# Scratch places by the plan's clock, new booked durations, and five weight halves with three raw blocks, in a hybrid decoder step

## The chip, the cores and the metric

The kernel runs on 1 core of one Trainium2 chip. The metric is device microseconds of one execution; lower is better. The engines are TensorE (PE in the profile, with its weight loads as PEld), VectorE (DVE), ScalarE (ACT), GpSimd (POOL), and SyncE (SP), which issues the DMA transfers here.

## The reference

One layer of a decoder, in float32, over 304 columns: 16 meta tokens, a prompt of 256 tokens, and 8 sequences of 4 new tokens each. Cut to what is computed:

```python
def decoder_layer(x, ...):
    xn = rms_norm(x, norm_mix)
    z = xn @ w_in                                  # 2048 -> 3360 RWKV columns + 4096 retention columns
    z_a, z_b = z[..., :RWKV_COLS], z[..., RWKV_COLS:]
    z_prev = concat([shift0, z_a[:, :-1]])
    o_a, S_a = rwkv7_mixer(z_a, z_prev, ...)       # 16 heads of 64, a state of 64x64 per head
    o_b, S_b = retention_mixer(z_b, ...)           # 4 heads of 256, a state of 256x256 per head
    h = x + concat([o_a, o_b]) @ w_out             # 2048 -> 2048
    hn = rms_norm(h, norm_ffn)
    return h + (silu(hn @ w_gate) * (hn @ w_up)) @ w_down    # 2048 -> 5632 -> 2048
```

A final norm follows. Returned are the outputs without the meta tokens, the last projected row, and both kinds of state, for the prompt and for each of the 8 sequences. The RWKV recurrence is solved in chunks of up to 64 tokens, the retention in chunks of 128, so both turn into many small matmuls between the large projections.

## The kernel before

**Projections.** Activations lie transposed, 128 channels on the partitions and up to 304 tokens along the row. Each projection is a list of output tiles of 128 columns, in the order that `sequence` (line 101) and `ORDER` give: the loras, then eight pairs of RWKV heads and four retention heads mixed, their gates, the output projection in two halves, then gate, up and down of the FFN. A tile sums over up to 16 steps of 128 rows. Every step is three matmuls in the rounded float32 format: high weight half by high activation half, high by low, low by high. They accumulate in one of two PSUM banks named `acc`; all other small matmuls write one of six banks named `mm`.

**Weights.** All weights are one array, `big`, packed in the order of use in raw blocks of 128 x 1024. `load` issues one block (512 KB) into a ring of `WR` buffers named `wr`; in `start` the first four blocks are issued as eight half blocks between the pieces of the input. `cast` rounds 512 columns on ACT to a tile `wh`, and `rest` lets DVE subtract that from the raw values to give `wl`; each of these has `WS` buffers. One half of 512 columns serves four steps, twelve matmuls. `main` (line 609 on) writes the steps of all projections in order; at each half it calls `load` until `WR` blocks from the present position are asked for, and `cast` until `WS - 1` halves from there are asked for:

```python
while self.loaded < min(total, at + WR * WCOLS):
    self.load()
while self.halved < min(total, at + (1 if starting else WS - 1) * 512):
    self.cast()
```

The subtracts are written at the middle of a half (`o == 256`), or at the next half's start if that half needs them.

**The planner.** The work between projections is written as generators (`mixed`, `pair`, `inverse`, `units`, `sample`, `pair_out`, `ret`, ...) that yield where they would wait. The program is written twice. The first pass is a draft: `Plan.book` gives every instruction a duration, follows values through tiles, and keeps a clock per engine; `Plan.pick` lets a generator take its next step once the clock of TensorE has passed the time when its last step was done. The choices are logged and replayed in the second pass, which writes the real program. So the booked durations set the order in which each engine's instructions stand, and each engine runs its list in order. `put` and `flush` issue output stores some 20 us of the plan's clock after they are asked for. The draft knows of the rings `wr`, `wh`, `wl`, `acc` and `mm` (`follows`), but gives each scratch tile words of its own.

**Scratch.** In the second pass all scratch tiles are pieces of two large tiles, the arenas, one of float32 and one of the rounded type (`arena_dt.float` and `arena_dt.float32r` in the profile). `Room` decides which words each tile gets. It notes for every tile the count of booked instructions when it was made and when it was last used; `pack` sorts the tiles by a key and gives each the lowest place that no tile with an overlapping life (longer by `slack` instructions) holds; `place` tries five keys, keeps the smallest room, and goes from a slack of 40 down to 0 until the room fits. Together the two rooms may hold 33,000 words per partition (`ROOM`), 4,200 of them of the rounded type. Where two tiles follow each other on the same words, the new owner's first instruction waits until the old owner's last reader is done. That holds for loads too, and SyncE issues its DMAs in order.

Every operation is recorded through one helper, so all rows of the profile name line 300; the tiles tell them apart.

Of the kernel before, what the change touches and what calls it, by code (L numbers as in the profile page):

```python
# [41 lines left out]
LATE = 20000  # L42
WARM = 10
BRIDGE = 4
WR = 4
WCOLS = 1024
WS = 4
PAIRS = 2
PMAX = 3
AHEAD = 2  # L50
# [25 lines left out]
KEYS = ((0, META, SEQ, 0), (P, P, NP - P, SEQ), (LASTK, 2 * P, T - 2 * P, SEQ + NP - P))  # L76
RMW = SEQ + NP - P + T - 2 * P
ROOM = 33000


def zcols():
# [223 lines left out]
class Plan:  # L305
# [5 lines left out]
    def __init__(self, nc, rooms, draft, log, keep):  # L311
        self.keep = keep
        self.rooms, self.draft, self.log, self.count = rooms, draft, log, 0
        self.clock = dict(PE=0.0, DVE=0.0, ACT=0.0, POOL=0.0, SP=0.0)
        self.end = self.dma = 0.0
        self.uses, self.outside = {}, ()
# [29 lines left out]
    def book(self, eng, what, a, k):  # L346
        self.count += 1
        if not self.draft:
            return
        aps = [x for x in (*a, *k.values()) if hasattr(x, "shape")]  # L350
        for x in aps:
            for room in self.rooms.values():
                room.use(x, self.count)
        out, ins = aps[0], aps[1:]

        at = 0.0
        boxes = [(x.name, self.box(x), x is out) for x in aps if x.name not in self.outside]
        meet = lambda a, b: a[0] < b[1] and b[0] < a[1] and a[2] < b[3] and b[2] < a[3]
        for name, box, writes in boxes:
            for other, done, by, written in self.uses.get(name, ()):  # L360
                if (written or writes) and done + 100 > at and not (by == eng == "PE") and meet(box, other):
                    at = max(at, done + (30 if by == eng else 100 if eng == "PE" else 60))
        n = math.prod(out.shape[1:])
        if eng == "PE":
            done = self.array(what, *a[:3], at) + 170
        elif eng == "SP":
            self.clock[eng] = at = max(self.clock[eng] + 400, at)
            self.dma = max(self.dma, at + 1400) + 4 * out.shape[0] * n / 320
            done = self.dma + 600
        else:  # L370
            part = out.shape[0] < P
            if eng == "DVE":
                big = max(math.prod(x.shape[1:]) for x in aps)
                dur, tail = {"stream_shuffle": (148, 90), "transpose": (95 + 1.02 * n, 80), "tensor_reduce": (40 + 1.8 * big, 85),
                             "tensor_tensor_scan": (65 + 2.1 * n, 85)}.get(what, (62 + 1.05 * n, 83))
            elif eng == "ACT":
                dur, tail = 108 + 0.83 * n, 94
            else:
                dur, tail = (60 + 0.85 * n, 60) if what == "memset" else (260 + 2.4 * n, 60)
            if part and eng != "POOL":  # L380
                dur += 110
# [72 lines left out]
class Room:  # L454

    def __init__(self):
        self.spans, self.index, self.places, self.size, self.taken = [], {}, None, 0, 0

    def note(self, ap, size, count):
        self.index[ap.name] = len(self.spans)
        self.spans.append([size, count, count])

    def use(self, x, count):
        i = self.index.get(getattr(x, "name", None))
        if i is not None:
            self.spans[i][2] = count

    def place(self, limit):  # L470


        for slack in (40, 20, 10, 5, 0):
            best = None
            for key in (lambda n, a, b: (-n, a), lambda n, a, b: (-n * (b - a), a), lambda n, a, b: (a - b, -n),
                        lambda n, a, b: (a, -n), lambda n, a, b: (-n // 256, a - b)):
                size, places = self.pack(key, slack)
                if best is None or size < best[0]:
                    best = size, places
            if best[0] <= limit:  # L480
                break
        self.size, self.places = best
        assert self.size <= limit, self.size

    def pack(self, key, slack):
        done, places = [], [0] * len(self.spans)
        for i in sorted(range(len(self.spans)), key=lambda i: key(*self.spans[i])):
            size, a, b = self.spans[i]
            size = -(-size // 8) * 8
            b += slack  # L490
            at = 0
            for o, n, c, d in sorted(x for x in done if x[2] <= b and a <= x[3]):
                if o - at >= size:
                    break
                at = max(at, o + n)
            places[i] = at
            done.append((at, size, a, b))
        return max(o + n for o, n, _, _ in done), places

    def take(self, size):  # L500

# [14 lines left out]
class Step:  # L516
# [33 lines left out]
    def t(self, shape, tag, dt=F32, bufs=None, pool=None):  # L550
        self.n += 1
        if pool is not None:
            name = f"{tag}_{self.n}"
            old = self.tags.setdefault(tag, [])
            old.append(name)
            n = {"mm": 8 - ACC, "acc": ACC}.get(tag, bufs)
            if n and len(old) > n:
                self.plan.follows(name, old[-1 - n])
            return pool.tile(shape, dt, tag=tag, name=name, **({} if bufs is None else {"bufs": bufs}))
        size = math.prod(shape[1:])  # L560
        if self.draft:
            ap = self.mp.tile(shape, dt, tag=f"t{self.n}", name=f"{tag}_{self.n}")
            self.rooms[dt].note(ap, size, self.plan.count)
            return ap
        o = self.rooms[dt].take(size)
        flat = self.arena[dt][:shape[0], o:o + size]
# [1145 lines left out]
def body(tc, I, O):  # L1712
# [32 lines left out]
```

## Time and profile before

| what | value |
|---|---|
| median of the runs | 1593.91 us (1592.52 to 1594.58, 3 runs) |
| the profiled execution's own time | 1595.29 us |
| its span, first to last instruction | 1593.5 us |
| mean granted clock of TensorE | 0.996 |
| busy: PE, DVE, ACT, POOL | 1547.0, 1101.9, 822.2, 166.5 us |
| moved by DMA | 252.49 MB, 158 GB/s on average |

Times in the profile are microseconds from the first instruction unless marked ns. A row of a group gives engine, operation, tiles written and read, shape and count, then busy time, mean ns of one, and the idle time of the engine just before them with what ended it. A row of waits reads: who waited, for whom, us in total, times, the longest. A row by stretches gives busy us and instruction counts of each engine, the granted clock, the busy share of the DMA engines and GB/s. Matmuls are pipelined, so the drawn length of one is longer than its distance to the next.

### The profile page before, as it was taken

The numbers are of one execution on the slowest core, as the hardware profiler recorded it, in microseconds if no ns is written. First come the engines' busy times: TensorE is split into PE (matmuls) and PEld (weight loads), VectorE is DVE, ScalarE is ACT, GpSimd is POOL, SyncE is SP. The second block draws the span as 40 slices with busy tenths as digits, with TensorE's granted clock in tenths as the row PEclk, the third lists the DMA queues.
The fourth block names the chain that finished last, engine by engine and source line by source line (L and its number), as shares of the span: only waits on it lengthen the run. The fifth ranks groups of instructions, "written<-read, shape, count | busy, mean of one in ns | idle before, by whom it ended". The sixth has DMA issues, their size and how long they took to land.

```text
span 1593.5 us, 30795 instructions
## 1 busy us (share of the span) xinstructions
PE 1547.0 (97%) x11388; PEld 1506.5 (95%) x11388; DVE 1101.9 (69%) x2590; ACT 822.2 (52%) x1795; POOL 166.5 (10%) x567
## 2 busy tenths in 40 slices
PE   9999999999999999999999999999999999999997
PEld 8888999898888899999999999999999999999997
DVE  7888888897879867777565656565655656565657
ACT  6657676747656564455444444444444444444445
POOL 0343414323041300000000000000000000000000
PEclk9999999999999999999999999999999999999998
DMA  7443343334543448655555555555555555555553
GB/s 263 144 123 112 114 126 113 101 113 133 157 156 117 143 149 278 231 163 157 169 164 165 168 170 159 169 166 168 166 166 172 160 165 167 172 162 170 162 168 116
DMA packets 76998, 252.49 MB, mean 158 GB/s; under 512 B 9392, under 2 KB 14640, under 8 KB 76848
## 3 DMA queue, kind: packets, MB, share of 16 engines
q1 hardware_dynamic: 76848, 250.52, 50.8%
q8 instruction: 90, 1.47, 0.4%
q14 instruction: 60, 0.49, 0.1%
HBM read 236.21 MB, written 14.28 MB: 157 GB/s over the span
## 4 chain that ended last, share of the span: by engine, by line
PE 71%; DVE 6%; DMA 2%; ACT 1%; issue 1%; POOL 1%; DVEq 0%; POOLq 0%; ACTq 0%; SPq 0%
PE acc L300 66%; PE mm L300 5%; DVE arena_dt.float L300 5%; DVE wl L300 1%; ACT arena_dt.float L300 1%; DMA arena_dt.float<-s0r 1%; POOL arena_dt.float L300 1%; DMA arena_dt.float<-lora 1%; DVE arena_dt.float32r L300 0%; ACT wh L300 0%; DVE xl L300 0%; ACT arena_dt.float32r L300 0%; DVEq L1741 0%; POOL shout L300 0%; POOLq L300 0%
## 5 line engine op out<-in xcount | busy, mean ns | idle before, releaser
L300 PE MATMUL acc<-xh,wh 128*128 128x288 f32 (+2 forms) x2592 | 791.7, 305 | 0.6 <-ACT wh L300 0.6
L300 PE MATMUL acc<-xh,wl 128*128 128x288 f32 (+2 forms) x2592 | 772.8, 298 | 13.3 <-DVE wl L300 13.2
L300 PE MATMUL acc<-xl,wh 128*128 128x288 f32 (+2 forms) x2592 | 766.8, 296 | 0.0
L300 ACT CAST wh<-wr 128x512 fp32r<-128x512 f32 x826 | 500.9, 617 | 363.8 <-PE acc L300 327.7
L300 DVE TENSOR_TENSOR wl<-wr,wh 128x512 fp32r<-128x512 f32 x826 | 562.8, 689 | 127.8 <-ACT wh L300 124.8
L300 PEld LDWEIGHTS acc<-xh,wl 128*128 128x128 f32 x2592 | 486.1, 188 | 19.7 <-DVE wl L300 18.9
L300 PEld LDWEIGHTS acc<-xh,wh 128*128 128x128 f32 x2592 | 487.8, 188 | 5.9 <-issue 1.3
L300 PEld LDWEIGHTS acc<-xl,wh 128*128 128x128 f32 x2592 | 486.9, 188 | 3.7 <-issue 0.5
L300 PE MATMUL acc<-arena_dt.float32r,wh 128*128 128x288 f32 x1408 | 280.0, 294 | 0.4 <-ACT arena_dt.float32r L300 0.3
L300 PEld LDWEIGHTS acc<-arena_dt.float32r,wh 128*128 128x128 f32 x1408 | 226.3, 188 | 0.9 <-ACT arena_dt.float32r L300 0.6
L300 PE MATMUL acc<-arena_dt.float32r,wl 128*128 128x288 f32 x704 | 208.0, 295 | 0.0
L300 DVE TENSOR_TENSOR arena_dt.float<-acc,arena_dt.float 128x288 f32<-128x288 f32 (+4 forms) x181 | 72.8, 420 | 167.1 <-PE acc L300 166.2
L300 PE MATMUL mm<-arena_dt.float 128*128 128x128 f32 (+6 forms) x1072 | 172.0, 311 | 15.4 <-ACT arena_dt.float L300 5.9
L300 PEld LDWEIGHTS mm<-arena_dt.float 128*128 128x128 f32 (+1 forms) x1072 | 138.1, 181 | 32.7 <-ACT arena_dt.float L300 8.5
L300 DVE TENSOR_TENSOR arena_dt.float<-arena_dt.float 128x288 f32<-128x288 f32 (+10 forms) x483 | 158.5, 355 | 10.8 <-ACT arena_dt.float L300 4.3
L300 DVE TENSOR_TENSOR arena_dt.float<-arena_dt.float,acc 128x288 f32<-128x288 f32 x208 | 94.4, 454 | 100.4 <-PE acc L300 99.9
L300 ACT ACTIVATE arena_dt.float<-arena_dt.float 128x288 f32<-128x288 f32 (+6 forms) x200 | 85.2, 433 | 122.7 <-DVE arena_dt.float L300 115.5
L300 ACT COPY arena_dt.float<-mm 64x64 f32<-64x64 f32 (+11 forms) x330 | 91.7, 286 | 80.6 <-PE mm L300 74.9
L300 PEld LDWEIGHTS acc<-arena_dt.float32r,wl 128*128 128x128 f32 x704 | 132.4, 188 | 0.0
L300 ACT CAST arena_dt.float32r<-arena_dt.float 128x288 fp32r<-128x288 f32 (+4 forms) x73 | 30.4, 423 | 124.2 <-DVE arena_dt.float L300 92.6
L300 POOL TENSOR_TENSOR arena_dt.float<-arena_dt.float 128x75 f32<-128x75 f32 (+14 forms) x240 | 86.9, 362 | 73.1 <-DVE arena_dt.float L300 50.1
L300 POOL MEMSET arena_dt.float<- 128x64 f32 (+8 forms) x137 | 29.7, 238 | 181.3 <-DVE arena_dt.float L300 102.9
(64 smaller groups left out, 675.5 us busy)
## 6 DMA issues: line engine op xcount, KB each, us to landing
wr<-big SPq DMA_DIRECT2D x409, 512.0 KB, 3.6
arena_dt.float<-s0r SPq DMA_DIRECT2D x16, 512.0 KB, 5.1
out_rts<-arena_dt.float SPq DMA_DIRECT2D x16, 512.0 KB, 5.6
arena_dt.float<-xT SPq DMA_DIRECT2D x4, 576.0 KB, 5.8
out_y<-arena_dt.float SPq DMA_DIRECT2D x8, 288.0 KB, 2.2
arena_dt.float<-xT SPq DMA_DIRECT2D x7, 304.0 KB, 6.2
wr<-big SPq DMA_DIRECT2D x8, 256.0 KB, 5.7
arena_dt.float<-lora SPq DMA_DIRECT2D x16, 128.0 KB, 3.5
```

The lines of the kernel that those rows point to most:

```text
L300: return self._plan.keep(f(*a, **k))
```

## The change

Four things change together.

1. **Places.** `Room` now keeps for each scratch tile the plan's times of its first and last use beside the counts; a life begins at the first use instead of when the tile is made. `pack` fits tiles into a given limit. For each tile it looks at the places that touch no tile alive at the same time, and takes the first place whose neighbours in time are at least `gap` ns of the plan's clock away, or else the one with the most time. `place` tries five keys with five gaps (2000 to 0 ns) and keeps the packing with the least `lack`, the sum over tiles of what is short of 800 ns. The limits stay: 4,200 words of the rounded type, `ROOM` for both.
2. **Durations.** `Plan.book` gets new durations: DVE `tensor_scalar` from SBUF 0.56 ns an element instead of 1.05, operands of one value per partition 67 ns (DVE) and 90 ns (ACT) each, ACT 40 ns less where it reads PSUM, a `tensor_copy` of POOL 185 + 0.8n instead of 260 + 2.4n ns and its other operations 265 + 2n, and 80 instead of 110 ns more for operations on part of the partitions.
3. **Halves.** `WS` goes from 4 to 5: five buffers each of `wh` and `wl` (2 KB a partition each), cast one half further ahead.
4. **Raw blocks.** `WR` goes from 4 to 3: three buffers of `wr` (4 KB a partition each), asked for one block less ahead. `start` still issues four blocks.

```diff
-WR = 4
+WR = 3
 WCOLS = 1024
-WS = 4
+WS = 5
...
 ROOM = 33000
+WIDE = 4200
+FREE, GAPS = 800.0, (2000.0, 1000.0, 500.0, 200.0, 0.0)
...
-        for x in aps:
-            for room in self.rooms.values():
-                room.use(x, self.count)
...
             part = out.shape[0] < P
+            each = sum(math.prod(x.shape[1:]) == 1 for x in ins) if n > 1 else 0
             if eng == "DVE":
                 big = max(math.prod(x.shape[1:]) for x in aps)
+                per = 0.56 if what == "tensor_scalar" and ins[0].name not in self.banks else 1.05
...
-                             "tensor_tensor_scan": (65 + 2.1 * n, 85)}.get(what, (62 + 1.05 * n, 83))
+                             "tensor_tensor_scan": (65 + 2.1 * n, 85)}.get(what, (62 + per * n + 67 * each, 83))
             elif eng == "ACT":
-                dur, tail = 108 + 0.83 * n, 94
+                dur, tail = 108 + 0.83 * n + 90 * each - 40 * (ins[0].name in self.banks), 94
             else:
-                dur, tail = (60 + 0.85 * n, 60) if what == "memset" else (260 + 2.4 * n, 60)
+                dur, tail = (60 + 0.85 * n, 60) if what == "memset" else (185 + 0.8 * n, 60) if what == "tensor_copy" else (265 + 2 * n, 60)
             if part and eng != "POOL":
-                dur += 110
+                dur += 80
...
+        for x in aps:
+            for room in self.rooms.values():
+                room.use(x, self.count, self.begun if eng == "PE" else self.clock[eng] - 400, done)
...
-    def use(self, x, count):
+    def use(self, x, count, at, done):
         i = self.index.get(getattr(x, "name", None))
-        if i is not None:
-            self.spans[i][2] = count
+        if i is None:
+            return
+        span = self.spans[i]
+        if span[1] is None:
+            span[1], span[3] = count, at
+        span[2], span[4] = count, max(span[4], done)
 
     def place(self, limit):
-        for slack in (40, 20, 10, 5, 0):
+        best = None
+        for key in (lambda n, a, b, *_: (-n, a), lambda n, a, b, *_: (-n * (b - a), a), lambda n, a, *_: (a, -n),
+                    lambda n, a, b, *_: (a - b, -n), lambda n, a, b, *_: (-n // 256, a - b)):
+            for gap in GAPS:
+                found = self.pack(key, limit, gap)
+                if found is not None and (best is None or found[0] < best[0]):
+                    best = found
+        self.lack, self.size, self.places = best
+
+    def pack(self, key, limit, gap):
+        done, places, lack, end = [], [0] * len(self.spans), 0.0, 0
+        used = [i for i, span in enumerate(self.spans) if span[1] is not None]
+        for i in sorted(used, key=lambda i: key(*self.spans[i])):
+            size, a, b, at, until = self.spans[i]
+            size = -(-size // 8) * 8
+            near = []
+            for o, n, c, d, s, u in done:
+                if a <= d and c <= b:
+                    near.append((o, o + n, -1.0))
+                else:
+                    free = max(0.0, at - u if d < a else s - until)
+                    if free < gap:
+                        near.append((o, o + n, free))
+            near.sort()
             best = None
...
+            for o in sorted({0, *(e for _, e, _ in near)}):
+                if o + size > limit:
                     break
...
+                free = min((f for s, e, f in near if s < o + size and o < e), default=gap)
+                if free > -1.0 and (best is None or free > best[0]):
+                    best = free, o
+                    if free >= gap:
+                        break
+            if best is None:
+                return None
+            lack += max(0.0, FREE - best[0])
+            places[i] = best[1]
+            end = max(end, best[1] + size)
+            done.append((best[1], size, a, b, at, until))
+        return lack, end, places
...
-    rooms[F32R].place(4200)
+    rooms[F32R].place(WIDE)
     rooms[F32].place(ROOM - rooms[F32R].size)
```

More of the change, by code (lines that the diff above doesn't have):

```diff
@@ L315, in __init__ @@
         self.end = self.dma = 0.0
-        self.uses, self.outside = {}, ()
+        self.uses, self.outside, self.banks = {}, (), set()
         self.mode, self.parts, self.empty, self.begun, self.idle = None, {}, 0.0, 0.0, 0.0
@@ L459, in __init__, with note @@
         self.spans, self.index, self.places, self.size, self.taken = [], {}, None, 0, 0
-    def note(self, ap, size, count):
+    def note(self, ap, size):
         self.index[ap.name] = len(self.spans)
-        self.spans.append([size, count, count])
-    def use(self, x, count):
+        self.spans.append([size, None, 0, 0.0, 0.0])
+    def use(self, x, count, at, done):
         i = self.index.get(getattr(x, "name", None))
-        if i is not None:
-            self.spans[i][2] = count
-    def place(self, limit):
-        for slack in (40, 20, 10, 5, 0):
-            best = None
[L475 to L493, printed above, removed]
-                    break
[L495 to L498, printed above, removed]
+        if i is None:
+            return
@@ L553, in t @@
             name = f"{tag}_{self.n}"
+            if tag in ("mm", "acc"):
+                self.plan.banks.add(name)
             old = self.tags.setdefault(tag, [])
@@ L562, in t @@
             ap = self.mp.tile(shape, dt, tag=f"t{self.n}", name=f"{tag}_{self.n}")
-            self.rooms[dt].note(ap, size, self.plan.count)
+            self.rooms[dt].note(ap, size)
             return ap
```

## The prediction

> **What bounds the kernel now.** I read the page first, then the busy times by stage, then who waits for whom in the first stage, then the chain of waits there.
>
> ```profile
> span 1593.5 us, 30795 instructions
> ...
> L300 PE MATMUL acc<-xh,wh 128*128 128x288 f32 (+2 forms) x2592 | 791.7, 305 | 0.6 <-ACT wh L300 0.6
> ```
>
> ```profile
> core 0: us, PE busy (x) PEld busy (x) DVE busy (x) ACT busy (x) POOL busy (x), PEclk, DMA share, GB/s
> 0.00:748.50 748.50, 713.30 (x5086) 673.74 (x5087) 600.73 (x1685) 459.80 (x1153) 166.51 (x567) 1.00 0.48 152
> 748.50:1578.00 829.50, 829.08 (x6269) 828.64 (x6269) 493.19 (x886) 361.51 (x641) 0.00 (x0) 1.00 0.54 164
> 1578.00:1593.50 15.50, 4.66 (x38) 4.14 (x36) 8.02 (x20) 0.89 (x2) 0.00 (x0) 0.65 0.41 161
> ```
>
> The profiled execution took 1595.29 us, its span 1593.5; 1.8 us lie around it. The median of the runs, 1593.91, is 1.4 us lower, and I take 1.4 off at the end. The FFN (748.5 to 1578) has TensorE busy for 829.08 of 829.50 us at 829.5/6269 = 132 ns a matmul: nothing to win there, and the tail of 15.5 us is not touched. So all gain must come from the first stage, the mixers and the output projection, where TensorE is idle for 748.5 - 713.3 = 35.2 us. That idle time is understated: a matmul is drawn 305 ns long though the next starts 132 ns after it, so each wait hides another 0.17 us. These are the waits in 0 to 748.5, TensorE's and then the weight loader's (the same waits, seen earlier in the pipe):
>
> ```profile
> PE acc L300 <- DVE wl L300: 13.2, 20, 1.2
> PE mm L300 <- ACT arena_dt.float L300: 6.8, 8, 1.7
> PE mm L300 <- POOL arena_dt.float L300: 4.6, 4, 1.6
> PE mm L300 <- DMA arena_dt.float<-s0r: 2.4, 5, 0.9
> PE mm L300 <- DVE arena_dt.float L300: 2.0, 4, 1.2
> ```
>
> ```profile
> PEld acc L300 <- DVE wl L300: 18.9, 24, 1.4
> PEld mm L300 <- ACT arena_dt.float L300: 10.5, 14, 2.0
> ...
> PEld mm L300 <- POOL arena_dt.float L300: 6.3, 6, 1.8
> PEld mm L300 <- DMA arena_dt.float<-s0r: 4.5, 5, 1.4
> ```
>
> There are two kinds. Matmuls of the projections wait for a low weight half (wl): 13.2 + 20 x 0.17 = 16.6 us by the one view, 18.9 by the other; I take **17**. Small matmuls wait for scratch written by ACT, POOL, DVE or a load: 15.8 us in 21 waits, + 21 x 0.17 = 19.4, against 21.3 in the other view; I take **20**.
>
> **Part 1, the places.** How much of the 20 us is a wait for a place and not for a value? Three rows name operations that have no value to wait for:
>
> ```profile
> L300 POOL MEMSET arena_dt.float<- 128x64 f32 (+8 forms) x137 | 29.7, 238 | 181.3 <-DVE arena_dt.float L300 102.9 <-PE mm L300 69.7 <-DVE arena_dt.float32r L300 6.4
> ```
>
> ```profile
> ACT arena_dt.float32r L300 <- DMA arena_dt.float<-lora: 31.4, 11, 5.2
> ```
>
> ```profile
> SPq L300 <- DVE arena_dt.float L300: 255.4, 61, 20.4
> ```
>
> A memset reads nothing, so nearly all of POOL's 181.3 us of idleness before the 137 memsets is waiting until DVE or TensorE had finished with the former owner of the words. A load reads HBM, and SyncE's queue stood 61 times for DVE's scratch work (some of these are stores, which wait for their data). ACT then stood 31.4 us at 11 late lora loads. One such case in the chain of waits, in order of time, and SyncE's issues around it:
>
> ```profile
> 292.63 0.87 DVE arena_dt.float L300 x3
> ...
> 293.57 2.20 DMA arena_dt.float<-lora
> ...
> 295.79 0.42 ACT arena_dt.float32r L300
> ...
> 296.57 0.66 DVE arena_dt.float L300 x3
> 297.24 0.19 POOL shout L300
> 297.43 0.16 POOL arena_dt.float L300
> ...
> 298.39 1.32 PE mm L300 x6
> ```
>
> ```profile
> 289.25 0.33 SPq L300 DMA_DIRECT2D wr<-big  x1
> 293.57 0.33 SPq L300 DMA_DIRECT2D arena_dt.float<-lora  x1
> 294.12 5.89 SPq L300 DMA_DIRECT2D wr<-big  x2
> ```
>
> DVE ends its work at 293.50, the load that follows it goes out at 293.57, and its value passes through ACT, DVE and POOL to a matmul at 298.39. The load could have gone any time after 289.6. The code agrees: the placing of before looks for the smallest room over a slack counted in instructions (40, 20, 10, 5, 0). The program's own draft ends it at slack 0 with 28,144 of 28,952 words, so words change hands at once everywhere, although the live words reach 27,563 only around the plan's 340 to 380 us and stay under 24,000 outside about 300 to 380. The new placing can use the whole room and asks for up to 2 us between owners. Removed: waits on former owners. Added: no instruction. The bounds of the share are 0 (all placings fall back to gap 0, or the value is late anyway) and 1; since loads and memsets show place as the cause directly, and ACT's waits only by inference, I take 0.65: **-13 us**. What is late next is the true chain, matmul to ACT copy to matmul.
>
> Stalls also cost clock. In one stretch TensorE idled and the granted clock fell below 1:
>
> ```profile
> 405.00:410.00 5.00, 3.19 (x14) 2.59 (x14) 4.38 (x10) 3.49 (x8) 0.21 (x1) 0.85 0.22 23
> 410.00:420.00 10.00, 10.00 (x66) 9.50 (x66) 8.47 (x23) 4.86 (x14) 0.91 (x5) 0.91 0.38 123
> ```
>
> That is 0.15 x 5 + 0.09 x 10 = 1.65 us, bounds 0 and 1.65 of gain; I take **-1**. The Trainium skill (TensorE: Matmul & The Clock Gate, section "What's actually happening") puts the half clock after an idle window of about 3.4 us. By that rule this stretch, idle for 5 - 3.19 = 1.81 us as drawn, should have kept its clock, and the term would be 0; the trace disagrees, and the trace decides.
>
> **Part 2, five pairs of halves (WS 5).** ACT casts and DVE subtracts run one half of 512 columns further ahead. How long is a half?
>
> ```profile
> L300 ACT CAST wh<-wr 128x512 fp32r<-128x512 f32 x305 | 183.2, 616 | 60.7 <-PE acc L300 53.6 <-DMA wr<-big 3.5 <-DVE arena_dt.float L300 1.3
> ```
>
> 748.5/305 = 2.45 us in the first stage. In the code the subtract for the half two ahead is written in the middle of a half, so wl had 1.5 halves (3.7 us) of lead and gets 2.5 (6.1 us). The longest wait, 1.4 us, is less than the 2.45 added, so all 17 us of wl waits could go. But DVE is busy 600.73 of 748.5 us and does the same work; where it is behind, the next small matmul stands instead. Bounds 0 and 17; halfway: **-8.5 us**. No instruction is added; casts move ahead of other ACT work by one half, 0.62 us each, hidden in ACT's idle 289 us.
>
> **Part 3, three raw blocks (WR 3).** The load of a block of two halves waits until the block three before (was four) is subtracted, and SyncE's queue stands there with the scratch loads behind it. Casting is one half earlier, so SyncE passes that point half a block sooner in the program, and the loads queued behind it are not later. What shrinks is the time from issue to cast: 7 halves before, 5 after.
>
> ```profile
> L300 SPq DMA_DIRECT2D wr<-big x23: 327/328/1031, 590.8 to 677.5; - x23
> ...
> DMA to landing us min/median/max: 3.4/4.8/8.2
> ```
>
> ```profile
> 750.00:1550.00 800.00, 343.20 (x506) 308.01 (x505) 1.00 0.55 166
> ```
>
> ```profile
> wr<-big SPq DMA_DIRECT2D x409, 512.0 KB, 3.6
> ```
>
> (the second row counts the work on raw blocks alone, DVE and ACT; the third is the page's, with the median landing). A half in the FFN takes 800/505 = 1.58 us. Three buffers turn once in 6 x 1.58 = 9.5 us. A turn holds the landing, one half until the second cast, that cast (0.62) and its subtract (0.69): landing + 2.9. So loads set the pace only from a landing of **6.6 us** on; the median is 3.6 us over the run and 4.8 us in 590 to 680, where states and stores move too. TensorE's total lead falls from 11 halves to 10. In 590 to 680 the worst is all 23 loads at 8.2: (8.2 + 2.9)/3 - 3.17 = 0.53 us each, 12 us; with medians it is 0. At the start of the run casting has one half of lead, so a late block can cost 0 to 3.6 - 1.58 = 2 us there; I take 1. Bounds 0 and 14, taken near the medians: **+1.5 us**.
>
> **Part 4, the durations.** They only change the order of the streams in the draft. Three rows against the booked time (duration and tail):
>
> ```profile
> L300 ACT COPY arena_dt.float<-mm 64x64 f32<-64x64 f32 x112 | 23.0, 205 | 11.9 <-PE mm L300 9.4 <-POOL arena_dt.float L300 0.7
> ...
> L300 POOL COPY arena_dt.float<-arena_dt.float 128x32 f32<-128x32 f32 x56 | 15.5, 307 | 29.6 <-DVE arena_dt.float L300 29.4
> ...
> L300 DVE TENSOR_SCALAR arena_dt.float<-arena_dt.float 128x288 int32<-128x288 int32 x24 | 7.4, 310 | 0.6
> ```
>
> The first was booked 365 and becomes 295, the second 397 and 271, the third 447 and 306. Two come closer; the POOL copy falls below its row. A better clock should lose less, a lighter one asks for matmuls sooner. I take **0**, bounds -8 and +8 (40% of the 20 us of small waits either way).
>
> **Sum.** 1595.3 - 13 - 1 - 8.5 + 1.5 = 1574.3 us in a profiled execution, 1573 as a median.
>
> **The rivals.** *Handed on*: the crowded stretch keeps gap 0 and a DVE behind its work makes the small matmuls wait instead. For it: DVE at 80%. Against: the crowd lasts some 80 us of 560. Half of the wl term, 2 us of places, 1.5 lost: -5, 1589 as median. *The change doesn't do what it says*: every packing with a gap fails at the peak (27,563 live of some 28,900 words), gap 0 is used, and the wl waits are handed on entirely: 1594. *Matmuls asked for too early* (the slower side): at 40 to 590 us the lighter clock writes small matmuls into TensorE's in-order queue before their inputs, and the projections behind them stand. These are all of the copies:
>
> ```profile
> L300 ACT COPY arena_dt.float<-mm 64x64 f32<-64x64 f32 (+11 forms) x330 | 91.7, 286 | 80.6 <-PE mm L300 74.9
> ```
>
> ```profile
> L300 POOL COPY arena_dt.float<-arena_dt.float 128x32 f32<-128x32 f32 (+5 forms) x123 | 35.3, 318 | 77.0 <-DVE arena_dt.float L300 70.4 <-ACT arena_dt.float32r L300 3.6 <-DMA out_rws<-arena_dt.float 2.3
> ```
>
> The price: 330 ACT copies booked up to 0.07 us shorter and 123 POOL copies 0.126 us shorter, 23 + 15 = 38 us. It decides from 21/38 = 55% of this on the path; at 80%, 1595.3 - 21 + 30 = 1604, 1603 as median. Against it: the ACT copy stays booked 90 ns above its row. *Late raw blocks*: the 14 us of part 3 while places give nothing and wl is handed on: 1608 as median; it needs landings above 6.6 us throughout, which no median shows.
>
> **How the numbers follow.** Forecast 66%, handed on 15%, no effect 7%, too early 8%, late blocks 4%. The forecast's own range joins shares of 0.3 and 1 for places (6 to 20), 4 to 17 for wl and the order's 8 either way, not all at one end: 1560 to 1587. To leave out 2 in 10 I take 1559 to 1591, which holds *handed on*. A measurement tells no less than 0.2%, 3.2 us. Faster: 66 + 12 of the 15 + 2 of the 7 = 80%; slower 12%; within 0.2% the other 8%.
>
> **What would show it.** Places: POOL's idleness before memsets falls from 181 to under 80 us, ACT's wait for lora loads from 31.4 to under 12, the small matmuls' waits (15.8) to under 8. Halves: the wl wait on TensorE under 5 us. Raw blocks: ACT's wait for raw loads in the first stage stays below 15 us and TensorE's idle time in the FFN below 1 us. The FFN starts near 728 and lasts 829 to 830. It is wrong if the FFN starts later than 743, if its length grows, or if small matmuls wait more than before.

## The result, and the profile after

The changed kernel takes 1558.88 us (median of 4 runs, 1557.57 to 1558.99) against 1594.24 us before: a ratio of 0.9777, 95% interval 0.976 to 0.9794. That is 35.4 us less, where 21 had been forecast. The time lies 0.1 us below the lower end of the range, 1559.

First the span and the busy times by stretches of the kernel after. The columns are those of the rows of before: each engine's busy us, then granted clock, busy share of the DMA engines, GB/s. The second row is an FFN stretch as in the prediction; the first ends where the first gate matmul starts.

```profile
span 1557.1 us, 30803 instructions
```

```profile
0.00:702.70 702.70, 691.97 (x5006) 662.96 (x5007) 592.39 (x1661) 453.15 (x1142) 179.24 (x567) 1.00 0.50 160
```

```profile
713.50:1541.50 828.00, 827.58 (x6258) 827.14 (x6258) 491.38 (x883) 360.18 (x637) 0.00 (x0) 1.00 0.54 165
1541.50:1557.10 15.60, 5.22 (x45) 4.78 (x43) 8.44 (x21) 1.52 (x3) 0.00 (x0) 0.77 0.41 159
```

The same stretch before, also up to its first gate matmul:

```profile
0.00:737.00 737.00, 702.92 (x5007) 663.59 (x5008) 591.54 (x1660) 453.92 (x1141) 166.51 (x567) 1.00 0.48 152
```

34.3 of the span's 36.4 us are gained before the first gate matmul. TensorE does the same 5006 or 5007 matmuls there, and its idle time falls from 34.1 us to 10.7. Its drawn busy time falls by another 11.0 us. Behind a wait matmuls are drawn with less overlap: TensorE has 12 waits there instead of 53, and 41 at the prediction's 0.17 us make 7 of the 11. The other 4 are not traced. The FFN still has TensorE busy for 827.58 of 828.00 us.

TensorE's and the weight loader's waits in the first 713.5 us (who waited for whom, us in all, times, longest):

```profile
PE mm L302 <- DVE arena_dt.float L302: 4.9, 5, 2.4
PE mm L302 <- ACT arena_dt.float L302: 1.6, 2, 0.9
...
PE acc L302 <- DVE wl L302: 0.8, 1, 0.8
PE mm L302 <- POOL arena_dt.float L302: 0.3, 1, 0.3
```

```profile
PEld mm L302 <- issue: 10.5, 27, 2.6
...
PEld acc L302 <- DVE wl L302: 1.5, 3, 1.0
PEld mm L302 <- ACT arena_dt.float L302: 1.5, 3, 0.9
```

The wl wait is as good as gone (13.2 us to 0.8 on TensorE), and the small matmuls wait 6.8 us for scratch instead of 15.8. Within these, the waits for scratch of DVE grew from 2.0 us to 4.9. The loader's longest row is now `issue`, time in which it waited for nothing that the profile shows: 10.5 us against 7.0 before. The rows that stood for waits on a place, in the same stretch:

```profile
L302 POOL MEMSET arena_dt.float<- 128x64 f32 (+8 forms) x137 | 28.6, 238 | 2.5 <-DVE arena_dt.float L302 0.7
```

```profile
ACT arena_dt.float32r L302 <- DMA arena_dt.float<-lora: 12.5, 5, 4.1
ACT wh L302 <- DMA wr<-big: 19.2, 12, 3.3
```

```profile
SPq L302 <- DVE wl L302: 430.0, 111, 12.9
SPq L302 <- DVE arena_dt.float L302: 146.3, 38, 12.5
```

The last row of before, in its first 748.5 us:

```profile
SPq L300 <- DVE arena_dt.float L300: 227.0, 52, 16.5
```

POOL stood 181.3 us before its memsets and now stands 2.5. SyncE's queue stands 38 times for DVE's scratch instead of 52. (The 61 times in the prediction are those of the whole run of before; the whole run after has 46.) ACT's wait for raw blocks has grown from 3.5 us to 19.2. One thing got worse: the clock. Three stretches of 5 us, in two places, have a granted clock below 1 (third column from the end), where before had one place of this kind:

```profile
10.00:15.00 5.00, 4.82 (x24) 4.72 (x24) 5.00 (x11) 5.00 (x11) 0.00 (x0) 0.66 1.04 399
...
365.00:370.00 5.00, 2.59 (x24) 1.65 (x26) 4.84 (x14) 2.31 (x6) 0.46 (x2) 0.89 0.99 326
370.00:375.00 5.00, 5.00 (x45) 3.51 (x38) 1.60 (x6) 2.40 (x10) 0.00 (x0) 0.76 0.49 173
```

The first costs 5 x 0.34 = 1.7 us, the other two together 5 x (0.11 + 0.24) = 1.75 us.

### The profile page after: what moved, and what is told of

The parts are those of the page before. It is cut to its first block, busy times and chain, and to the rows that moved or that the text cites. A ratio compares the mean times of both kernels' runs of the same rounds, so it can differ in the third digit from the quotient of the medians.

```text
span 1557.1 us, 30803 instructions
## 1 busy us (share of the span) xinstructions
PE 1535.6 (99%) x11388; PEld 1505.7 (97%) x11388; DVE 1102.0 (71%) x2590; ACT 821.4 (53%) x1795; POOL 179.2 (12%) x567
## 4 chain that ended last, share of the span: by engine, by line
PE 85%; DVE 11%; issue 1%; ACT 1%; DMA 1%; POOL 0%; SPq 0%; DVEq 0%; ACTq 0%; POOLq 0%
PE acc L302 76%; PE mm L302 9%; DVE arena_dt.float L302 8%; DVE wl L302 3%; ACT arena_dt.float L302 1%; DMA arena_dt.float<-xT 0%; POOL arena_dt.float L302 0%; DMA arena_dt.float<-lora 0%; ACT wh L302 0%; DVE arena_dt.float32r L302 0%; DMA wr<-big 0%; ACT arena_dt.float32r L302 0%; SPq L302 0%; DVEq L1766 0%; ACT xh L302 0%
## 5 line engine op out<-in xcount | busy, mean ns | idle before, releaser
L302 PE MATMUL mm<-arena_dt.float 128*128 128x128 f32 (+7 forms) x1072 | 168.4, 317 | 6.2 <-DVE arena_dt.float L302 4.9
L302 DVE TENSOR_TENSOR arena_dt.float<-arena_dt.float 128x288 f32<-128x288 f32 (+11 forms) x483 | 159.5, 354 | 11.7 <-ACT arena_dt.float L302 6.2
L302 ACT COPY arena_dt.float<-mm 64x64 f32<-64x64 f32 (+8 forms) x330 | 91.1, 287 | 72.6 <-PE mm L302 62.4
L302 POOL TENSOR_TENSOR arena_dt.float<-arena_dt.float 128x75 f32<-128x75 f32 (+14 forms) x240 | 94.5, 394 | 100.4 <-DVE arena_dt.float L302 75.6
L302 POOL COPY arena_dt.float<-arena_dt.float 128x32 f32<-128x32 f32 (+5 forms) x123 | 35.6, 321 | 125.9 <-DVE arena_dt.float L302 74.0
```

What stands on the lines that cost most here:

```text
L302: return self._plan.keep(f(*a, **k))
```

## The experiments

The theory to be tested was the prediction's sum: places 13 us, the lead of the halves 8.5, raw blocks and durations about nothing. Its main rival, once the result was known, was that the places did nearly all of it. All runs are medians against the kernel before on the same chip, 1593.9 to 1595.1 us. Where two changed kernels are compared, their medians stand as measured, some of them on different chips; since the kernel before differs by 1.2 us between those, a difference of 2 us or less says little.

### The places alone, and the change without time between uses

`places_alone` keeps every engine's list of before, instruction by instruction, and changes only the words. With that order the new `pack` fits only at gap 0, because the peak of live words is too high. So here tiles that live where more than 25,000 words are alive take gap 0, and the others up to 2 us.

```diff
+CROWD = 25000
...
+        live = np.zeros(max(span[2] for span in self.spans) + 1)
+        for i in used:
+            live[self.spans[i][1]:self.spans[i][2] + 1] += self.spans[i][0]
+        full, want = live > CROWD, gap
...
+            gap = 0.0 if full[a:b + 1].any() else want
```

> The kernel before, with every engine's list of instructions in the same order; only the scratch places differ: packed with gaps up to 2 us wherever fewer than 25,000 words are alive, gap 0 in the crowd. Theory 'places' (waits on former owners are the bulk of the 35 us): 1564 to 1574 us, POOL's idleness before memsets far down, small matmuls' waits on TensorE under 8 us of 15.8. Theory 'halves' (the wl lead is the bulk): 1582 to 1592. Theory 'order' (the new clock and rings write a better order): 1585 to 1594.

`gap0` is the changed kernel, its order unchanged, with no time asked for between owners.

```diff
-FREE, GAPS = 800.0, (2000.0, 1000.0, 500.0, 200.0, 0.0)
+FREE, GAPS = 800.0, (0.0,)
```

> The changed kernel, every engine's list in the same order; all packings forced to gap 0, so words change hands at once. Theory 'places': 1578 to 1590 us (25 to 30 us of the gain lost). Theory 'halves': 1562 to 1570. Theory 'order': 1559 to 1568.

Measured: `places_alone` 1564.71 us, ratio 0.9818 (0.9803 to 0.9832). `gap0` 1610.98 us, ratio 1.0102 (1.0083 to 1.0122). Of `places_alone`, the stretch up to its first gate matmul at 705.8, then the loader's and TensorE's waits in the first 717 us:

```profile
0.00:705.80 705.80, 694.63 (x5007) 661.88 (x5008) 589.64 (x1660) 453.53 (x1141) 179.75 (x567) 1.00 0.50 159
```

```profile
PEld acc L303 <- DVE wl L303: 8.5, 16, 1.4
PEld mm L303 <- ACT arena_dt.float L303: 4.9, 7, 1.4
...
PEld mm L303 <- DMA arena_dt.float<-s0r: 2.6, 4, 1.1
...
PEld mm L303 <- POOL arena_dt.float L303: 0.5, 2, 0.3
```

```profile
PE acc L303 <- DVE wl L303: 4.4, 10, 1.1
```

Of `gap0`, TensorE's waits in the first 762 us, the memsets, and one pair of stretches:

```profile
PE mm L302 <- ACT arena_dt.float L302: 16.5, 12, 3.0
PE mm L302 <- DVE arena_dt.float L302: 9.3, 7, 2.8
...
PE acc L302 <- DVE wl L302: 1.9, 5, 0.7
```

```profile
L302 POOL MEMSET arena_dt.float<- 128x64 f32 (+8 forms) x137 | 29.6, 238 | 181.6 <-DVE arena_dt.float L302 116.0 <-ACT arena_dt.float L302 41.2 <-PE mm L302 18.5
```

```profile
75.00:80.00 5.00, 3.10 (x15) 2.54 (x14) 3.17 (x7) 4.22 (x11) 3.48 (x19) 0.82 0.61 190
80.00:85.00 5.00, 5.00 (x33) 4.76 (x33) 2.25 (x5) 2.47 (x7) 0.00 (x0) 0.84 0.07 26
```

What follows: with the order of before, the places alone are worth 30 us of the 35, with not one instruction moved. Both kinds of waits fall. On the weight loader those for scratch of ACT, POOL and loads go from 21.3 us to 8.0, and the wl waits go from 18.9 to 8.5, on TensorE from 13.2 to 4.4. No cast, no subtract and no ring differs between the two kernels, so over half of the loader's wl waits, 10.4 of 18.9 us, came from the words. How they did is argued, not traced: the casts and subtracts stand in the lists of ACT and DVE behind scratch work, and scratch work waited for its place. One case of before shows such a list at work. DVE stands 1.16 us for POOL until 318.88, does five shuffles, and starts a subtract at 319.65; TensorE's wait of 0.80 us for that wl ends at 320.43. Whether a place or a value held POOL up there, the trace doesn't say. In `gap0` the halves have their lead and the wl wait stays at 1.9 us. Yet the small matmuls wait 25.8 us for ACT and DVE, and the kernel is 16 us slower than before, where the changed one is 35 faster. That lies above all three ranges named for it; even 'places' had expected at most 1590. The order that the new draft writes, run with words handed on at once, is worse than the old order. Seven lapses of the clock like the one shown make 7 x 1.7 = 12 us of its time.

### The rings alone

`rings_alone` is the kernel before with the two sizes changed; the old placing then stops at a slack of 10 instructions, where before had to go down to 0. `rings_tight` holds it at 0. (This is the float32 arena. The smaller arena of the rounded type stops at a slack of 5 in before and of 10 in `rings_alone`, and `rings_tight` holds it at 0 too.)

```diff
-WR = 4
+WR = 3
...
-WS = 4
+WS = 5
```

```diff
-        for slack in (40, 20, 10, 5, 0):
+        for slack in (0,):
```

> The kernel before with five pairs of halves and three raw blocks alone, old places and durations. Theory 'places': 1586 to 1594 us, the wl wait on TensorE under 5 us but the small matmuls wait more. Theory 'halves': 1565 to 1575. Theory 'order': between, 1580 to 1590.

> Rings alone, as in rings_alone, same order of every engine's list, but the old placing is held at slack 0 (in rings_alone its draft let it stop at slack 10, in the kernel before at slack 0). Theory 'places' (rings alone won mainly because the old placing could keep 10 instructions of distance): 1585 to 1605 us, at least 13 us above rings_alone's 1571.6. Theory 'halves' (the lead won it): 1568 to 1576. POOL's idleness before memsets would go from 115 back to 150 to 190 us under 'places' and stay near 115 under 'halves'.

Measured: 1571.64 us, ratio 0.9851 (0.9837 to 0.9866), and 1582.84 us, ratio 0.9924 (0.9909 to 0.9938). Half of what the rings give alone, 11.2 of 23.4 us, is really places: the draft that knows of them leaves more room. The 11.2 lie between the ranges of the two theories, so neither is right alone.

### The lead of the halves by itself

Two kernels separate the order that a draft writes from the rings that the real program uses. `lead_alone` is `places_alone` with the draft made for four blocks and four halves and the program for three and five. `order_alone` is the changed kernel (with the finer gaps below) with the draft for three and five and the program for four and four; its edit has the two pairs below swapped.

```diff
+        self.wr, self.ws = (4, 4) if draft else (3, 5)
...
-                while self.loaded < min(total, at + WR * WCOLS):
+                while self.loaded < min(total, at + self.wr * WCOLS):
...
-                while self.halved < min(total, at + (1 if starting else WS - 1) * 512):
+                while self.halved < min(total, at + (1 if starting else self.ws - 1) * 512):
```

> The run places_alone, all scratch work in the same order and the same places, but with three raw blocks and five pairs of halves in the real program only (the draft keeps four and four): only casts, subtracts and raw loads move ahead. Theory 'lead' (the wl lead itself is worth something once places are free): 1557 to 1561 us, the wl wait on TensorE from 3.2 to under 1 us. Rival 'order' (the rings win by the order that their draft writes): 1563 to 1566.

> The run finer_gaps, all scratch work in the same order and places, but with four raw blocks and four pairs of halves in the real program only. Theory 'lead': 1566 to 1576 us, 8 us or more of wl waits on TensorE. Rival 'order': 1556 to 1560.

Measured: `lead_alone` 1556.92 us, ratio 0.977 (0.9755 to 0.9784), 7.8 below `places_alone`. `order_alone` 1576.57 us, ratio 0.9889 (0.9874 to 0.9904), 20.0 above the same order with five halves. The loader's wl wait of `order_alone`, in 0 to its first gate matmul at 716.2:

```profile
PEld acc L302 <- DVE wl L302: 14.7, 27, 1.2
```

And of the same order and words with five halves (`finer_gaps`), to its first gate matmul at 698.2:

```profile
PEld acc L302 <- DVE wl L302: 1.6, 3, 1.0
```

So the lead, with one raw block less, is worth about 8 us in the old order and about 20 in the new one. Both times lie just beyond the range named for 'lead', on the side of the larger effect.

### Three raw blocks, and two

`places_durations` is the changed kernel with four blocks and four halves; `places_durations_wr3` has the same order and words and three blocks. `two_raw_blocks` has two, five halves, the finer gaps and 1,000 more words for scratch, which two blocks leave free.

```diff
-WR = 3
+WR = 4
...
-WS = 5
+WS = 4
```

```diff
-WS = 5
+WS = 4
```

```diff
-WR = 3
+WR = 2
...
-ROOM = 33000
+ROOM = 34000
```

> The changed kernel with the rings of before (four raw blocks, four pairs of halves): new places and durations only; its packing falls short by 7 us in all against 286 us in the changed kernel. Theory 'places': 1558 to 1567 us, so the rings add little once places are free. Theory 'halves': 1567 to 1575, with 8 us or more of wl waits on TensorE.

> The run before it with three raw blocks for four, all else the same (the draft, the order and the packing come out alike): the price of the fourth block alone. By part 3 of the prediction 0 to 3 us slower than with four, and ACT's wait for raw loads in the first stage under 15 us. Rival (late raw blocks): 8 to 14 us slower.

> As finer_gaps with two raw blocks instead of three, and the 1,024 words this frees given to the float32 room (its packing then falls short of 800 ns nowhere). Part 3's count gives two buffers a turn of 6.3 us, so loads would set the pace from a landing of 3.4 us on, which the median of 3.5 exceeds. If that count is right: the FFN alone grows by 20 us or more, 1575 us and above. If casting's lead hides it: 1553 to 1558.

Measured: 1575.99 us, ratio 0.9877 (0.9862 to 0.9892); 1575.79 us, ratio 0.9878 (0.9863 to 0.9893); 1578.66 us, ratio 0.9905 (0.9885 to 0.9924). ACT's wait for raw blocks in the first 720 us, of the first two kernels in turn:

```profile
ACT wh L302 <- DMA wr<-big: 1.0, 1, 1.0
```

```profile
ACT wh L302 <- DMA wr<-big: 24.6, 12, 4.8
```

And of `two_raw_blocks`, up to its first gate matmul at 720.7 and behind it, with the FFN's busy times:

```profile
ACT wh L302 <- DMA wr<-big: 137.1, 77, 4.0
```

```profile
ACT wh L302 <- DMA wr<-big: 224.3, 142, 3.6
```

```profile
720.70:1563.10 842.40, 840.76 (x6352) 839.73 (x6352) 510.62 (x913) 359.33 (x657) 0.00 (x0) 1.00 0.54 165
```

`places_durations` lies above both of its ranges; the section on the durations comes back to it. Going from four blocks to three makes ACT wait 24 us more and costs TensorE nothing. With two blocks TensorE is still busy for 840.76 of 842.40 us in the FFN, although ACT stands 224 us for loads behind the first gate matmul: ACT is busy for 359 us of this stretch, and casting runs four halves ahead. The same 842.4 us from the first gate matmul on hold 6352 TensorE matmuls here and 6351 in `finer_gaps`, so the FFN is no slower. The loss of some 22 us falls in the first stage, where ACT also serves the small matmuls; 5.1 us of it are clock lost in three lapses, where `finer_gaps` has none. The time of 1578.66 us is what I had expected if the turn of two buffers set the pace of the FFN, but it did not come about in that way.

### The durations

`durations_alone` is the kernel before with the new durations, where the old placing stops at a slack of 20; `durations_tight` holds it at 0 (the edit of `rings_tight`). `places_rings` is the changed kernel with the old durations.

```diff
-                dur, tail = (60 + 0.85 * n, 60) if what == "memset" else (185 + 0.8 * n, 60) if what == "tensor_copy" else (265 + 2 * n, 60)
+                dur, tail = (60 + 0.85 * n, 60) if what == "memset" else (260 + 2.4 * n, 60)
...
-                dur += 80
+                dur += 110
```

> The kernel before with the new booked durations alone, old places and rings: only the order of the streams changes. Theories 'places' and 'halves': 1588 to 1600 us. Theory 'order': 1572 to 1584.

> As durations_alone (1586.5 us), same order of every engine's list, with the old placing held at slack 0; in durations_alone its emptier draft let it stop at slack 20. Theory 'better packing' (the new durations won only by the distance that the packing could keep): 1594 to 1610 us. Theory 'better order': 1583 to 1590.

> The changed kernel with the old booked durations: new places and rings; its packing falls short by 6 us in all. If the new durations help once places are free (as between the kernel before and durations_alone): 1562 to 1570 us, above finer_gaps. If they only won through a better packing: 1554 to 1560.

Measured: 1586.49 us, ratio 0.9943 (0.9924 to 0.9961); 1614.41 us, ratio 1.012 (1.01 to 1.0141); 1553.7 us, ratio 0.9746 (0.973 to 0.9763). The 8.5 us that the durations seem to bring alone come from the emptier scratch that their draft leaves: held at a slack of 0, their order costs 19 us, more than the range for 'better packing' allowed. (The arena of the rounded type, at 5 in before, is at 0 here too, so this comparison is a little unfair to the order.) The change without them is 5.2 us faster than the change.

`finer_gaps` has the changed kernel's order with 14 gaps to choose from, among them 900, 800, 700 and 600; `pack` then ends 3 us short of 800 ns over all tiles, where the five gaps left 286. Two more kernels take parts of the durations back, with four blocks, four halves and the finer gaps: POOL's (`no_pool_durations`), and ACT's reading of PSUM with the part figure (`no_psum_durations`). `no_pool_ws5` takes POOL's back with three blocks and five halves.

```diff
-FREE, GAPS = 800.0, (2000.0, 1000.0, 500.0, 200.0, 0.0)
+FREE, GAPS = 800.0, (2000.0, 1500.0, 1000.0, 900.0, 800.0, 700.0, 650.0, 600.0, 550.0, 500.0, 400.0, 300.0, 200.0, 0.0)
```

```diff
-                dur, tail = (60 + 0.85 * n, 60) if what == "memset" else (185 + 0.8 * n, 60) if what == "tensor_copy" else (265 + 2 * n, 60)
+                dur, tail = (60 + 0.85 * n, 60) if what == "memset" else (260 + 2.4 * n, 60)
```

```diff
-                dur, tail = 108 + 0.83 * n + 90 * each - 40 * (ins[0].name in self.banks), 94
+                dur, tail = 108 + 0.83 * n + 90 * each, 94
...
-                dur += 80
+                dur += 110
```

> The changed kernel, same order of every engine's list, with fourteen gaps to try in place of five: the best packing is short of 800 ns by 3 us over all tiles in place of 286 us. Theory 'places' with gains still open: 1552 to 1557 us. If 500 ns between owners is already enough: 1557 to 1560, no difference.

> As places_durations (1576.0 us, four raw blocks, four pairs of halves, free places) with POOL's old booked times and the rest of the new. If POOL's copies, booked below their rows, ask for matmuls too early: back towards places_alone, 1563 to 1569. If not: 1572 to 1580.

> As places_durations with the old booked times for ACT reads of PSUM (no 40 ns less) and for operations on part of the partitions (110 ns more, not 80), POOL new. If these lighter figures ask for matmuls too early: 1563 to 1569. If not: 1572 to 1580.

> The changed kernel with three raw blocks, five halves and the finer gaps, all new durations kept but POOL's, which are booked as before. With four halves POOL's booked times made 7.6 us of the 11 us that the new durations cost. If POOL's times are the fault here as well, this gives back most of the 3 us between the finer gaps (1556.6) and the old durations (1553.7): 1552 to 1555. If the cost lies in the other durations, or was an effect of four halves only: 1556 to 1558. A packing 7.2 us of the plan's time short of 800 ns in all is no cause for a difference (3 us and 5.9 us in the two it stands between).

Measured: 1556.56 us, ratio 0.9755 (0.9739 to 0.9771); 1568.41 us, ratio 0.9833 (0.9818 to 0.9848); 1575.31 us, ratio 0.9877 (0.9861 to 0.9894); 1550.87 us, ratio 0.9725 (0.9709 to 0.9741). The span of the last, and TensorE's waits in its first 700 us:

```profile
span 1549.4 us, 30805 instructions
```

```profile
PE mm L302 <- DVE arena_dt.float L302: 2.1, 5, 0.7
...
PE mm L302 <- ACT arena_dt.float L302: 0.6, 1, 0.6
PE mm L302 <- POOL arena_dt.float L302: 0.5, 1, 0.5
```

So the new durations are two things. POOL's make the kernel 5.7 us slower with five halves (1556.6 against 1550.9) and about 7.6 with four; the others make it 2.8 us faster (1553.7 to 1550.9). The PSUM and part figures make no difference that can be told (1575.3 against 1576.0, with four halves). `no_pool_ws5` is the fastest kernel, 8.0 us below the changed one and just below the range named for POOL's fault. Why POOL's lighter clock costs that much stays open: no single row of waits carries the 5.7 us.

## Why the prediction was right or wrong

**What bounds the kernel** was right: 34.3 of the span's 36.4 us came from ahead of the FFN, from TensorE's idle time there and the waits' share that is drawn as overlap.

**Part 1, the places**, is the step that failed, and in one place. It applied the share to the 20 us of small waits alone, and the prediction put the 17 us of wl waits under the halves. The small waits were right: 21.3 us on the loader became 8.0, 13.3 gone against 13 forecast, though the share of 0.65 was a choice between 0 and 1 and so in part luck. But 10.4 us of the loader's wl waits went with the places too. The clock kept at 1 in the first stage, which is another 1.7. That makes 25.4 of the 30 us that `places_alone` measured where 13 and 1 stood, and where the bound for the places was 20. The other 5 us lie in small rows of the loader, whose waits fell from 59.3 us to 29.2 in all. The largest of them, of before and of `places_alone`:

```profile
PEld mm L300 <- issue: 7.0, 14, 1.5
```

```profile
PEld mm L303 <- issue: 3.9, 13, 0.6
```

The prediction read a wait by the tile that it names: scratch was a sign of places, wl a sign of too short a lead. It did not ask what the subtract itself had been waiting behind. That the time missed the range by only 0.1 us is luck: the range allowed at most 20 us for the places and reached its low end with the halves and the order, for which it allowed up to 25 together. In the changed kernel itself the clock's term came out with the other sign: two lapses instead of one, +1.7 us where -1 was forecast.

**Part 2, the halves**, at 8.5 us was right in size, by luck: `lead_alone` measured 7.8. These are not half of 17 us. The places leave 8.5 us of this wl wait to the loader, and `lead_alone` has none of it left. As the prediction feared, some is handed on: TensorE's wait for DVE's scratch rises from 0.8 us to 5.9, while its waits for ACT's scratch and the loads fall from 3.5 to 0.9.

**Part 3, the raw blocks**, at +1.5 measured -0.2 (the two kernels with four halves), within what can be told. The sign named for it, ACT's wait for raw loads below 15 us, was wrong: 19.2 us. It was a poor sign, because that wait lies beside TensorE's work. The landing of 6.6 us that was to set the pace is a doubtful test too: by the same count two blocks would set it from 3.4 us on, the median landing in `two_raw_blocks` is 3.5, and the FFN is no slower there. That is only just beyond the count's limit, so it doesn't settle where TensorE would feel late blocks.

**Part 4, the durations**, at 0 within 8 either way: 2.9 us of loss with five halves (`finer_gaps` against `places_rings`), but 11.3 with four (`places_durations` against `places_alone`, whose rules for the gap differ). The prediction's worry, the POOL copy that falls below its row, points at the right engine; the runs took all of POOL's figures back at once, so they don't single out the copy.

**The sum, made again from the runs**: 1594.2 - 30.3 (places, against the 1595.0 us of before beside it) - 7.8 (lead) - 3.2 (a draft that knows the rings, `lead_alone` to `places_rings`) + 2.9 (durations) + 2.3 (five gaps instead of 14) = 1558.1, measured 1558.9. Each step is the difference of two neighbouring runs, so that the sum closes is no proof. It says how the gain divides along this path; along another the steps are worth other sums, as the lead shows. The last three are about as small as a measurement can tell, and the step from `lead_alone` to `places_rings` also changes the rule for the crowd.

**The rivals.** *Late raw blocks* fell. *Handed on* fell as the main account, and is there in the small: the waits for DVE's scratch above. *The change doesn't do what it says* was right on half of its ground: with the order of before every gap does fail at the peak. It did not come about, because the drafts with the new rings or durations leave room for gaps (500 ns in the changed kernel's float32 arena); and its price was wrong, for `gap0` costs 1611 us, not 1594. *Asked for too early* may be there in the small: the durations cost the 3 us above, not 30, and why they cost them is open.

**The signs.** Memset idleness under 80 us (2.5), small waits under 8 (6.8), the wl wait under 5 (0.8) and an FFN with under 1 us idle (0.42) came as said; lora waits under 12 just missed (12.5). The first gate matmul starts at 702.7; the 748.5 that the prediction called the start of the FFN lies 11.5 us behind that matmul of before, so its 728 answers to 716 and was too late by 14.

## What to carry to other kernels

When tiles share words, add up every wait that a reused place can cause, also those that reach the busy engine through another engine's in-order list: a row that names a value (a weight half) can be a place at one remove. Give a packer time between uses, not instruction counts, and check with the gap taken away what an order is worth: the same order was 16 us slower or 35 us faster than before by its places alone. Booked durations that come closer to the rows one by one need not give a better order; try them one engine at a time.

## What the runs showed of the hardware

**A stall has a second price.** In the first stage the lapses of the granted clock cost 1.7 us each: one in before, seven in `gap0`, two in the kernel after, none in `places_alone`, `finer_gaps` and `no_pool_ws5`. In `rings_alone` one lasts twice as long, from 472 to 479 us, and costs 3.4. The first lapse of the kernel after, and what lies ahead of it, by single us:

```profile
8.00:9.00 1.00, 0.32 (x3) 0.08 (x1) 0.00 (x0) 0.56 (x2) 0.00 (x0) 1.00 1.01 383
9.00:10.00 1.00, 0.45 (x2) 0.30 (x2) 0.98 (x2) 1.00 (x3) 0.00 (x0) 1.00 1.05 411
10.00:11.00 1.00, 0.82 (x5) 0.72 (x5) 1.00 (x3) 1.00 (x3) 0.00 (x0) 0.77 1.05 410
11.00:12.00 1.00, 1.00 (x6) 1.00 (x6) 1.00 (x3) 1.00 (x3) 0.00 (x0) 0.50 1.04 404
12.00:13.00 1.00, 1.00 (x6) 1.00 (x6) 1.00 (x3) 1.00 (x3) 0.00 (x0) 0.50 1.06 407
13.00:14.00 1.00, 1.00 (x6) 1.00 (x6) 1.00 (x3) 1.00 (x3) 0.00 (x0) 0.52 0.98 372
```

TensorE is idle for 0.68 + 0.55 + 0.18 = 1.4 us, in pieces, and then has half its clock for 0.23/0.5 + 1 + 1 + 0.48/0.5 = 3.4 us. The Trainium skill (TensorE: Matmul & The Clock Gate, section "What's actually happening") describes a gate of two settings, full and half, that judges by windows of 3413 ns which run on regardless of the program. The trace agrees in the length of a lapse, 3.4 us, and in the 0.50. It disagrees with the idle window that the section asks for, since 1.4 us of scattered idleness, as drawn, was enough here. How little is enough, no run here fixes. Two lapses, 3.4 us, that the finer places don't have, can account for the 2.3 us between the five gaps and the 14.

**ACT hides what it waits for.** 224 us of waiting for raw blocks on ACT in the FFN of `two_raw_blocks` left TensorE with 1.6 us of idle time in 842.4.

**The same POOL instructions got slower.** `places_alone` runs the list of before on POOL, but its tensor-tensor operations took 382 ns on average instead of 362. The rows of before and of that kernel:

```profile
L300 POOL TENSOR_TENSOR arena_dt.float<-arena_dt.float 128x75 f32<-128x75 f32 (+14 forms) x240 | 86.9, 362 | 73.1 <-DVE arena_dt.float L300 50.1
```

```profile
L303 POOL TENSOR_TENSOR arena_dt.float<-arena_dt.float 128x75 f32<-128x75 f32 (+14 forms) x240 | 91.6, 382 | 90.9 <-DVE arena_dt.float L303 69.0
```

Only words and start times differ between the two. Which of them does it was not tried; in `places_alone` POOL has 0% of the chain that ended last.
